# A decoder trunk on one core: low parts of the weights by accumulating transfers, and 17 convolution taps from TensorE to VectorE

## The chip, the core and the metric

The kernel runs on one core of a Trainium2 chip. A core has TensorE for matrix products, VectorE, ScalarE and GpSimd for element-wise work, and SyncE, which here issues transfers; each engine takes its own instructions in order and waits on semaphores. Sixteen DMA engines move data between memory and the on-chip buffer. The metric is the device time of one execution in microseconds, as the median of several runs.

## What is computed

The input is a stream of 512 tokens of 1024 channels, in float32. The first layer is a conformer convolution module and a gated feed-forward, the second an attention with three dilated windows and a feed-forward of the same shape. The conformer module is what the change touches beside the weights:

```python
u = h @ w_in + b_in
u = u[..., :D_MODEL] * jax.nn.sigmoid(u[..., D_MODEL:])
u = causal_dwconv(u, dw, dw_b)        # depthwise, 31 taps
u = layer_norm(u, ln_g, ln_b)         # over the 1024 channels
u = jax.nn.silu(u)
return u @ w_out + b_out
```

Around each module stands a norm before and a norm after with a residual add. The feed-forward has a width of 2816, with a depthwise convolution of three taps; the attention has 8 heads of 128 in each of the three branches.

## The kernel before

**Products.** Activations lie with channels on partitions and tokens along the row. To keep float32 accuracy each operand is split into a high part, rounded to the format of TensorE's fast pass (`F32R`), and a low part, the remainder. A product of x and w is then three products on TensorE: xh·wh, xl·wh and xh·wl (`mm3`), each of 128 × 128 weights with 512 or 256 columns. In names `hh`, `hl` are high and low part of a normed chunk, `sh`, `sl` of the conformer's activated chunk, `whi`, `wlo` of a weight.

**Weights.** The weights come in 240 units of 128 × 1024, in the order of use. `loader` issues a unit's load from SyncE into one of two buffers `raw`, as soon as the low part of the unit two before it has been made. `splitter` makes the high part with a copy on ScalarE and the low part with a subtraction `raw − whi`, on VectorE or on GpSimd, whichever has it sooner by a rough clock; chains of statistics (`self.chains`) keep it off GpSimd. High and low parts have seven buffers each (`RING`), and the splitter runs up to six units (`AHEAD`) before the one in use. Some units are held while their products come in several passes: those of the conformer's output product, of the attention's output product `w_o`, and of a part of the feed-forward. The first two units come in pieces and have their own code (`first_units`).

**Order of the work.** The program is written out by a planner at build time: TensorE's stream leads, and chains of other work (generators) join when a model clock (`Clock`) says that their operands stand. The result is one fixed order for each engine.

**The conformer.** Six of its eight channel chunks are convolved whole, three by banded blocks on TensorE (`T` are the blocks, which GpSimd builds) and three with chains of taps over several engines (`ca`, `cb`, `cacc`). The last two chunks (`MIXES`, 6 and 7) are done in two token halves, in `mix`: of the 30 taps beside the current token, the first 17 of chunk 6 and the first 20 of chunk 7 (`MIX_PE`) are products on TensorE with diagonal matrices (`dh`, `dl`, built by ScalarE; sums in `cm`), three products of 256 columns for each tap and half; the other taps are chained multiply-adds on VectorE (`mc`, 128 × 256 each). Two additions per half bring in the mean `nm` and the products' sum `cm`.

Layer norm follows. `stat_acc` adds three convolved chunks on GpSimd to `m`; TensorE sums its columns (`st`), and the mean, broadcast into `nm`, centres each chunk on VectorE (`d`). The sums of centred values and squares are gathered on GpSimd (`s`), TensorE sums over channels (`lst`), VectorE and GpSimd make the scale (`lnr`), TensorE broadcasts it (`bc`), and VectorE (`ln`, `sl`) and ScalarE (`sh`) make the operands of the output product `wo`. It runs half by half: a0 is the first half of the first four output chunks, b0 their second half.

**Junctions.** Between two modules (`Junction`) the output chunks `y` are squared and summed, a norm is broadcast, and for each chunk VectorE makes `t`, the new residual `x` and the low part `hl`, ScalarE the high part `hh` and squares `sq`, which GpSimd and VectorE add.

The functions that the change touches follow; other functions lost only a comment line.

Of the kernel before, what the change touches and what calls it, by code (L numbers as in the profile page):

```python
# [10 lines left out]
F32 = mybir.dt.float32  # L11
# [14 lines left out]
NEG = -1e30  # L26
RING = 7
AHEAD = 6
SEGS = [list(range(0, 6)), list(range(6, 14)), list(range(14, 22))]
# [3 lines left out]
MIXES = (6, 7)  # L33
MIX_PE = (17, 20)
MAIN_BANKS = 7
TURN = 8
SLACK = 0.3
POOL_BIAS = -1
# [111 lines left out]
class When:  # L150
    """The next step may go once its operands stand and the engine is about to be free."""

# [4 lines left out]
class Meter:  # L157
    """Passes calls on to an engine and keeps a rough clock of when their results stand."""

# [22 lines left out]
class Clock:  # L182
# [55 lines left out]
    def op(self, kind, name, a, k):  # L238
# [3 lines left out]
        if name == "dma_start":  # L242
# [7 lines left out]
            self.free["dma"] = s + n / 360e3  # L250
            fin = self.free["dma"] + 0.9
        else:
# [40 lines left out]
class Junction:  # L293
    """Post-norm, residual add and the operands of the next phase, one token half at a time."""

# [13 lines left out]
    def evict(self, m, p, ap, sl, mode, bias=None, sq=True, after=None, tag=0):  # L309
        """A finished chunk of y leaves PSUM; its squares are summed."""  # L310
        b, nc = self.b, self.b.nc
# [130 lines left out]
class Builder:  # L442
    def __init__(self, tc, ctx, x_d, w_d, vec_d, cvec_d, const_d, out_d):
# [47 lines left out]
        nc.sync.dma_start(self.X[0], x_d[0])  # L491
        self.raw01 = [self.wp.tile([128, 1024], F32, tag="raw", name=self.name("raw"), bufs=2) for _ in range(2)]
        for i, (o0, o1) in enumerate(PIECES):
# [6 lines left out]

    # ---- order of emission: the tensor engine's stream leads, chains of other work join when they are due
    @property
# [47 lines left out]
    def step(self, what):  # L550
        """The main stream waits: time goes on to the next chain that is due."""
        assert self.sides, what
        t = min(s.due(self.clock) for s in self.sides)
        self.now = max(self.now, t)
        assert self.now < self.t + 1000.0 and self.now < 5000.0, what
        self.advance(self.pick(max(t, self.t)))
# [6 lines left out]
    def hold_for(self, *aps):  # L563
        """Chains that are due before the operands stand go first."""
        while self.sides:
            t = self.clock.ready(*aps)
            d = min(s.due(self.clock) for s in self.sides)
            if self.t >= t or d >= t:
                break
            self.step("hold")  # L570
# [4 lines left out]
    def warm(self, out, n):  # L575
        """Products of zeros before the first real ones: the tensor engine's clock is gated down while it idles."""
        for _ in range(n):
            self.nc.tensor.matmul(out[:, :256], self.zero[:, :128], self.zero, start=True, stop=True)

    # ---- tiles  # L580
    def name(self, s):
# [36 lines left out]

    # ---- weights
    def hold(self, specs):  # L620
        """These units stay open until they are released: their products come in several passes."""
        self.held |= {self.index[s] for s in specs}
# [13 lines left out]
    def loader(self):  # L636
        nc = self.nc
        late = [(self.cst0, self.const_d[:, :160]), (self.vec, self.vec_d[:, NVA:]), (self.cst, self.const_d[:, 160:])]
        for u in range(2, len(self.order)):
            yield from self.until(("lo", u - 2))  # L640
            yield At(self.lo_done[u - 2])
            w = self.width(u)
            self.raw[u] = raw = self.wp.tile([128, 1024], F32, tag="raw", name=self.name("raw"), bufs=2)
            self.clock.hold("sp", self.lo_done[u - 2])
            nc.sync.dma_start(raw[:, :w], self.w_d[u, :, :w])
            self.mark(("raw", u))
            if u >= LATE and late:
                nc.sync.dma_start(*late.pop(0))

    def splitter(self):  # L650
        """High parts come from the Activation engine, low parts from whichever of two engines has them sooner."""
        nc, free = self.nc, self.clock.free
        for u in range(2, len(self.order)):
            while u > self.cur + AHEAD or u - RING >= self.oldest or ("raw", u) not in self.flags:
                yield 0.1
            self.next_unit = u
            raw, w = self.raw.pop(u), self.width(u)
            yield When("act", max(self.clock.ready(raw[:, :w]), self.unit_done.get(u - RING, 0.0)), SLACK)
            hi = self.wp.tile([128, 1024], F32R, tag="whi", name=self.name("whi"))
            lo = self.wp.tile([128, 1024], F32R, tag="wlo", name=self.name("wlo"))  # L660
            self.clock.hold("act", self.unit_done.get(u - RING, 0.0))
            nc.scalar.copy(hi[:, :w], raw[:, :w])
            yield self.rdy(hi[:, :w])
            at = self.clock.ready(hi[:, :w])
            if not self.chains and max(free["pool"], at) + w / 476.0 + POOL_BIAS < max(free["dve"], at) + w / 960.0:
                eng = nc.gpsimd
            else:
                eng = nc.vector
                yield self.when("dve", hi[:, :w])
            eng.tensor_tensor(lo[:, :w], raw[:, :w], hi[:, :w].bitcast(F32), op=ALU.subtract)  # L670
            self.lo_done[u] = self.clock.ready(lo[:, :w])
            self.split[self.order[u]] = (hi, lo)
            self.mark(("lo", u))
# [4 lines left out]
    def first_units(self, i):  # L678
        """One piece of the first two units, whose loads are cut so that the first products start early."""
        nc = self.nc  # L680
# [18 lines left out]

    # ---- products  # L700
    def mm3(self, out, wh, wl, xh, xl, start, stop):
# [52 lines left out]

    # ---- statistics
    def sums(self, p, o, accs, blocks):
# [5 lines left out]
    def stat(self, r, acc, blocks, rest=None):  # L762
        """r = (mean square + eps) ** -0.5 of the tokens in the blocks."""
        nc, nb = self.nc, len(blocks)
# [25 lines left out]

    # ---- conformer module
    def conv_taps(self, w_idx, Ts):
        """Banded blocks of the depthwise kernel for tokens taken four at a time."""
        nc = self.nc
# [123 lines left out]
    def stat_acc(self, CO, L):  # L918
        """Sums of the centred channels and of their squares, chunk by chunk as they come."""
        nc = self.nc  # L920
# [362 lines left out]

    # ---- feed-forward
    def ffn(self, layer, Jin, Jout):
# [95 lines left out]

    # ---- attention
    def proj_evict(self, g, p, R, t):
# [330 lines left out]
    def reload(self, src):  # L1714
        """The residual stream comes back from memory: its place was needed for other things."""
        self.X = [self.c2("x") for _ in range(KC)]
# [8 lines left out]
class Chunks:  # L1725
    """Operand pairs looked up when they are needed."""

# [109 lines left out]
```

## Time and profile before

| what | value |
| --- | --- |
| median of 3 runs | 1523.62 us (1523.43 to 1525.43) |
| span of the profiled execution | 1520.0 us |
| the profiled execution's own time beside its span | the page gives none |
| TensorE busy | 1484.2 us, 98% |
| VectorE busy | 941.5 us, 62% |
| ScalarE busy | 603.5 us, 40% |
| GpSimd busy | 355.7 us, 23% |
| loads on SyncE's queue | 135.38 MB |

A busy share is a mean over stages with different limits. The chain of waits goes back from the last instruction to what released it at each step, so it shows which engine set the end where. A row of the timeline gives the start, the time, the instruction with output and inputs, and in brackets the idle time before it with what ended it. In the profile every instruction has the line of the helper that records it (L168), so rows are told apart by engine and by the names of their tiles.

### The profile page before, as it was taken

What the parts mean: (1) busy time and instruction counts of PE and PEld (TensorE: products, weight loads), DVE (VectorE), ACT (ScalarE), POOL (GpSimd) and SP (SyncE); (2) the same over time, 40 slices, a digit from 0 to 9 for tenths busy, and PEclk for the clock granted to TensorE, in tenths of its full rate; (3) what the DMA queues carried; (4) which work ended last, traced back from release to release, by engine and by line L of the source; (5) the groups of instructions that cost most, each with busy time, mean ns of one, the idle gap of its engine ahead of it and who ended that gap; (6) DMA issues with size and microseconds to landing.
All of it is one profiled execution on the core that took longest, in us unless ns stands there. A gap on an engine that the chain in (4) does not pass through costs nothing.

```text
span 1520.0 us, 19689 instructions
## 1 busy us (share of the span) xinstructions
PE 1484.2 (98%) x7778; PEld 1277.0 (84%) x7778; DVE 941.5 (62%) x1366; ACT 603.5 (40%) x1020; POOL 355.7 (23%) x231
## 2 busy tenths in 40 slices
PE   7999999999999998999999999999999999999997
PEld 5889998888888888889888889888898888888887
DVE  7997867846754757722655622566568746754745
ACT  5465564443432425424222323233356334422423
POOL 5885223301210216300000000000044302210213
PEclk9999999999999999999999999999999999999998
DMA  5430322233232322432222232222222332322311
GB/s 183 159 105 29 98 84 84 87 122 97 92 101 84 97 70 86 143 106 96 70 77 77 70 97 84 81 73 70 97 84 84 97 125 84 97 97 91 101 45 56
DMA packets 46892, 139.78 MB, mean 92 GB/s; under 512 B 5072, under 2 KB 10960, under 8 KB 46800
## 3 DMA queue, kind: packets, MB, share of 16 engines
q1 hardware_dynamic: 42768, 135.38, 27.4%
q10 hardware_dynamic: 4032, 3.15, 0.7%
q8 instruction: 61, 1.00, 0.3%
q14 instruction: 31, 0.25, 0.1%
HBM read 132.74 MB, written 5.77 MB: 91 GB/s over the span
## 4 chain that ended last, share of the span: by engine, by line
PE 83%; DVE 5%; ACT 1%; issue 1%; POOL 1%; DMA 0%; POOLq 0%; DVEq 0%; ACTq 0%
PE fi L168 31%; PE kq L168 17%; PE fo L168 16%; PE v L168 9%; PE wo L168 5%; PE sc L168 2%; DVE hl L168 1%; DVE mc L168 1%; DVE x L168 1%; PE pw L168 1%; PE pt L168 1%; PE pv L168 1%; DVE t L168 1%; PE cim L168 1%; PE st L168 0%
## 5 line engine op out<-in xcount | busy, mean ns | idle before, releaser
L168 ACT CAST whi<-raw 128x1024 fp32r<-128x1024 f32 (+2 forms) x242 | 248.2, 1027 | 552.8 <-PE fi L168 175.4
L168 POOL TENSOR_TENSOR wlo<-raw,whi 128x1024 fp32r<-128x1024 f32 (+1 forms) x79 | 190.8, 2416 | 985.8 <-ACT whi L168 975.6
L168 DVE TENSOR_TENSOR wlo<-raw,whi 128x1024 fp32r<-128x1024 f32 (+2 forms) x163 | 206.8, 1269 | 169.0 <-ACT whi L168 168.4
L168 PE MATMUL fi<-hl,whi 128*128 128x512 f32 (+1 forms) x768 | 289.9, 377 | 2.2 <-DVE hl L168 2.2
L168 PE MATMUL fi<-hh,whi 128*128 128x512 f32 (+1 forms) x768 | 290.8, 379 | 0.0
L168 PE MATMUL fi<-hh,wlo 128*128 128x512 f32 (+1 forms) x768 | 289.6, 377 | 0.0
L168 PEld LDWEIGHTS fi<-hl,whi 128*128 128x128 f32 x768 | 145.5, 189 | 31.4 <-DVE hl L168 2.6
L168 PEld LDWEIGHTS fi<-hh,wlo 128*128 128x128 f32 x768 | 145.5, 189 | 28.7
L168 PEld LDWEIGHTS fi<-hh,whi 128*128 128x128 f32 x768 | 145.6, 190 | 28.5
L168 PE MATMUL kq<-hh,whi 128*128 128x512 f32 (+1 forms) x416 | 164.5, 396 | 0.0
L168 PE MATMUL kq<-hh,wlo 128*128 128x512 f32 (+1 forms) x416 | 156.9, 377 | 0.0
L168 PE MATMUL kq<-hl,whi 128*128 128x512 f32 (+1 forms) x416 | 156.7, 377 | 0.0
L168 PE MATMUL fo<-uh,whi 128*128 128x512 f32 (+1 forms) x416 | 150.1, 361 | 0.0
L168 PE MATMUL fo<-uh,wlo 128*128 128x512 f32 (+1 forms) x416 | 149.7, 360 | 0.0
L168 PE MATMUL fo<-ul,whi 128*128 128x512 f32 (+1 forms) x416 | 149.7, 360 | 0.0
L168 DVE SCALAR_TENSOR_TENSOR cc<-z,vec,cc 128x511 f32<-128x511 f32 (+1 forms) x176 | 139.4, 813 | 7.0 <-ACT cc L168 4.3
L168 DVE TENSOR_TENSOR z<-fi,R 128x512 f32<-128x512 f32 x88 | 60.2, 689 | 98.3 <-PE fi L168 96.2
L168 PEld LDWEIGHTS kq<-hh,wlo 128*128 128x128 f32 x416 | 78.3, 188 | 15.5
L168 DVE TENSOR_TENSOR kq<-kq,R 128x512 f32<-128x512 f32 x48 | 46.1, 969 | 70.0 <-PE kq L168 69.3
L168 PEld LDWEIGHTS fo<-ul,whi 128*128 128x128 f32 x416 | 78.3, 188 | 13.1
L168 PEld LDWEIGHTS fo<-uh,whi 128*128 128x128 f32 x416 | 78.3, 188 | 13.0
L168 DVE TENSOR_TENSOR ul<-cc,uh 128x512 fp32r<-128x512 f32 x44 | 75.0, 1705 | 22.7 <-ACT uh L168 22.5
(212 smaller groups left out, 2631.6 us busy)
## 6 DMA issues: line engine op xcount, KB each, us to landing
raw<-in_w_dram SPq DMA_DIRECT2D x222, 512.0 KB, 3.5
raw<-in_w_dram SPq DMA_DIRECT2D x18, 384.0 KB, 3.1
x<-in_x_dram SPq DMA_DIRECT2D x16, 256.0 KB, 4.4
xs<-x SPq DMA_DIRECT2D x8, 256.0 KB, 2.7
x<-xs SPq DMA_DIRECT2D x8, 256.0 KB, 5.1
out_dram<-x SPq DMA_DIRECT2D x16, 128.0 KB, 1.8
ud<-u ACTq DMA_DIRECT2D x3, 256.0 KB, 2.0
ug<-ud ACTq DMA_DIRECT2D x3, 256.0 KB, 3.3
```

Source lines behind the costliest of these rows:

```text
L168: return f(*a, **k)
```

## The change

The low part of a unit is made in another way. ScalarE writes the negative rounded weight, −1 × raw into `wlo`, and copies the rounded weight into `whi` as before; GpSimd then issues a transfer from `raw` to `wlo` that adds what it brings onto what lies there. The buffers for raw weights are four instead of two. Of the diagonal taps 9 and 11 stay on TensorE, where 17 and 20 were; VectorE has 40 taps per half of a chunk pair instead of 23. The model clock gets another figure for transfers issued by GpSimd, which moves the order that it writes. Comment lines that were taken out are not shown.

```diff
+RAWS = 4
-MIX_PE = (17, 20)
+MIX_PE = (9, 11)
...
@@ Clock.op @@
-            fin = self.free["dma"] + 0.9
+            fin = self.free["dma"] + (0.9 if kind != "pool" else 2.0)
...
@@ loader @@
         for u in range(2, len(self.order)):
-            yield from self.until(("lo", u - 2))
-            yield At(self.lo_done[u - 2])
+            if u >= RAWS:
+                yield from self.until(("lo", u - RAWS))
+                yield At(self.lo_done[u - RAWS])
             w = self.width(u)
-            self.raw[u] = raw = self.wp.tile([128, 1024], F32, tag="raw", name=self.name("raw"), bufs=2)
-            self.clock.hold("sp", self.lo_done[u - 2])
+            self.raw[u] = raw = self.wp.tile([128, 1024], F32, tag="raw", name=self.name("raw"), bufs=RAWS)
+            self.clock.hold("sp", self.lo_done.get(u - RAWS, 0.0))
             nc.sync.dma_start(raw[:, :w], self.w_d[u, :, :w])
...
@@ splitter @@
+            nc.scalar.activation(lo[:, :w], raw[:, :w], AF.Copy, scale=-1.0)
             nc.scalar.copy(hi[:, :w], raw[:, :w])
-            yield self.rdy(hi[:, :w])
-            at = self.clock.ready(hi[:, :w])
-            if not self.chains and max(free["pool"], at) + w / 476.0 + POOL_BIAS < max(free["dve"], at) + w / 960.0:
-                eng = nc.gpsimd
-            else:
-                eng = nc.vector
-                yield self.when("dve", hi[:, :w])
-            eng.tensor_tensor(lo[:, :w], raw[:, :w], hi[:, :w].bitcast(F32), op=ALU.subtract)
+            yield self.when("pool", lo[:, :w], slack=0.0)
+            nc.gpsimd.dma_start(lo[:, :w], raw[:, :w], accum_op=ALU.add)
```

What that does to the order is seen in three places. The first place is GpSimd's row at the layer norm of the conformer's second half, where `s` are the sums, `lnr` the scale and `wlo` the weights. Before:

```order
L168 TENSOR_TENSOR s_225_1121<-s_225_1121,sq_1432 128x512
L168 TENSOR_TENSOR s_224_1120<-s_224_1120,mc_962 128x256
L168 TENSOR_TENSOR s_225_1121<-s_225_1121,mq_963 128x256
L168 TENSOR_TENSOR lnr_1509<-lnv_1506,mhalf 128x2
L168 TENSOR_TENSOR wlo_1527<-raw_1036,whi_1526 128x1024
L168 TENSOR_TENSOR wlo_1573<-raw_1500,whi_1572 128x1024
```

And now:

```order
L169 DMA wlo_1400<-raw_842 128x1024
L169 TENSOR_TENSOR s_225_1112<-s_225_1112,d_1357 128x512
L169 TENSOR_TENSOR s_226_1113<-s_226_1113,sq_1422 128x512
L169 DMA wlo_1444<-raw_886 128x1024
L169 TENSOR_TENSOR s_225_1112<-s_225_1112,mc_1010 128x256
L169 TENSOR_TENSOR s_226_1113<-s_226_1113,mq_1011 128x256
L169 DMA wlo_1485<-raw_981 128x1024
L169 TENSOR_TENSOR lnr_1520<-lnv_1517,mhalf 128x2
L169 DMA wlo_1754<-raw_1167 128x1024
```

Issues stand between the sums and ahead of the scale, where subtractions stood behind it. In the same way 12 issues stand ahead of `m` on GpSimd, where four subtractions were.

The second place is TensorE around the sums of the second half, with `wo` the output product and `st`, `lst`, `bc` the sums and the broadcast; in the first listing `sh_1729` is a chunk of the first half, and the sums `lst` stand among products further up, the last 18 of them ahead of the broadcast. Before:

```order
L168 MATMUL wo_1819<-sh_1729,wlo_779 128x256
L168 MATMUL wo_1820<-sh_1729,whi_884 128x256
L168 MATMUL wo_1820<-sl_1730,whi_884 128x256
L168 MATMUL wo_1820<-sh_1729,wlo_885 128x256
L168 MATMUL bc_1928<-cst_75,lnr_1913 128x128 x4
L168 MATMUL wo_1821<-sh_1729,whi_980 128x256
L168 MATMUL wo_1821<-sl_1730,whi_980 128x256
L168 MATMUL wo_1821<-sh_1729,wlo_981 128x256
L168 MATMUL wo_1822<-sh_1729,whi_1472 128x256
L168 MATMUL wo_1822<-sl_1730,whi_1472 128x256
```

And now, with `sh_1738` the last chunk of the first half and `sh_1591` the first of the second:

```order
L169 MATMUL wo_1675<-sh_1738,whi_1399 128x256
L169 MATMUL wo_1675<-sl_1739,whi_1399 128x256
L169 MATMUL wo_1675<-sh_1738,wlo_1400 128x256
L169 MATMUL lst_1850<-ones,s_225_1112 128x1 x2
L169 MATMUL lst_1850<-ones,s_226_1113 128x1 x2
L169 MATMUL lst_1863<-ones,mc_1015 128x1 x2
L169 MATMUL lst_1863<-ones,mq_1016 128x1 x2
L169 MATMUL bc_1876<-cst_75,lnr_1873 128x128 x4
L169 MATMUL wo_1672<-sh_1591,whi_816 128x256
```

Products of the first half stood between the sums and behind the broadcast, 30 of them behind it (6 of this chunk and 24 of the two that follow); now all of them stand ahead of the sums, and b0 follows the broadcast at once.

The third is VectorE at the end of the second half's taps, `mc` of the two chunks, with `nm` and `cm` the mean and the diagonal products. Before:

```order
L168 SCALAR_TENSOR_TENSOR mc_962<-mu_959,vec,mc_962 128x256
L168 TENSOR_TENSOR mc_962<-mc_962,nm_1107 128x256
L168 TENSOR_TENSOR mc_962<-mc_962,cm_1609 128x256
L168 SCALAR_TENSOR_TENSOR mc_967<-mu_964,vec,mc_967 128x256 x3
L168 TENSOR_TENSOR mc_967<-mc_967,nm_1107 128x256
L168 TENSOR_TENSOR mc_967<-mc_967,cm_1695 128x256
L168 TENSOR_SCALAR lns_330_1892<-lst_1877 128x4
```

And now:

```order
L169 SCALAR_TENSOR_TENSOR mc_1010<-mu_1007,vec,mc_1010 128x256
L169 SCALAR_TENSOR_TENSOR mc_1015<-mu_1012,vec,mc_1015 128x256
L169 TENSOR_TENSOR mc_1010<-mc_1010,nm_1098 128x256
L169 TENSOR_TENSOR mc_1010<-mc_1010,cm_1533 128x256
L169 SCALAR_TENSOR_TENSOR mc_1015<-mu_1012,vec,mc_1015 128x256 x5
L169 TENSOR_TENSOR mc_1015<-mc_1015,nm_1098 128x256
L169 TENSOR_TENSOR mc_1015<-mc_1015,cm_1584 128x256
L169 TENSOR_SCALAR lns_324_1857<-lst_1850 128x4
```

The end of the row is the same; ahead of it 17 more taps alternate between the two chunks.

## Rows read from the trace of the kernel before

**Rows 1.** The page, part 1: busy time of the engines

```profile
PE 1484.2 (98%) x7778; PEld 1277.0 (84%) x7778; DVE 941.5 (62%) x1366; ACT 603.5 (40%) x1020; POOL 355.7 (23%) x231
```

**Rows 2.** The page, costliest groups: busy us, mean ns, idle before

```profile
L168 ACT CAST whi<-raw 128x1024 fp32r<-128x1024 f32 (+2 forms) x242 | 248.2, 1027 | 552.8 <-PE fi L168 175.4
L168 POOL TENSOR_TENSOR wlo<-raw,whi 128x1024 fp32r<-128x1024 f32 (+1 forms) x79 | 190.8, 2416 | 985.8 <-ACT whi L168 975.6
L168 DVE TENSOR_TENSOR wlo<-raw,whi 128x1024 fp32r<-128x1024 f32 (+2 forms) x163 | 206.8, 1269 | 169.0 <-ACT whi L168 168.4
```

**Rows 3.** Chain of waits: start us, us, what

```profile
144.64 1.15 PE lst L168 x8
...
180.60 29.54 PE wo L168 x246
...
211.60 1.23 DVE wlo L168
...
226.59 0.94 ACT whi L168
...
339.64 89.23 PE fi L168 x384
...
1136.96 3.00 DVE hl L168 x2
```

**Rows 4.** Windows: length; busy PE, PEld, DVE, ACT, POOL; granted clock, DMA share, GB/s

```profile
164.00:177.00 13.00, 12.21 (x100) 11.71 (x99) 12.45 (x25) 4.49 (x10) 4.24 (x3) 1.00 0.28 102
226.00:228.00 2.00, 0.10 (x1) 0.00 (x0) 2.00 (x5) 2.00 (x5) 0.01 (x1) 1.00 0.01 4
232.00:234.00 2.00, 2.00 (x11) 2.00 (x11) 1.63 (x6) 0.00 (x0) 0.69 (x1) 0.50 0.07 27
```

**Rows 5.** Timeline of GpSimd: start us, us, instruction, idle before

```profile
44.21 2.41 POOL L168 TENSOR_TENSOR wlo<-raw,whi 128x1024 fp32r<-128x1024 f32 x1 [2.20 <-PE cig L168]
...
64.28 6.05 POOL L168 TENSOR_TENSOR T<-cst,cv 128x512 f32<-128x512 f32 x5 [2.67 <-DMA cv<-in_cvec_dram]
...
107.39 1.51 POOL L168 TENSOR_TENSOR m<-m,co 128x512 f32<-128x512 f32 x1
...
178.59 0.71 POOL L168 TENSOR_TENSOR lnr<-lnv,mhalf 128x2 f32<-128x2 f32 x1 [3.05 <-DVE lnv L168]
```

**Rows 6.** Timeline of VectorE: the same columns

```profile
113.64 1.09 DVE L168 TENSOR_TENSOR d<-co,nm 128x512 f32<-128x512 f32 x1 [1.12 <-issue]
...
124.48 3.53 DVE L168 SCALAR_TENSOR_TENSOR mc<-mu,vec,mc 128x230 f32<-128x230 f32 x9
...
141.09 0.42 DVE L168 TENSOR_TENSOR mc<-mc,cm 128x255 f32<-128x255 f32 x1
...
150.73 1.08 DVE L168 TENSOR_TENSOR ln<-d,bc 128x256 f32<-128x256 f32 x3 [1.29 <-PE bc L168]
...
176.40 0.42 DVE L168 TENSOR_TENSOR mc<-mc,cm 128x256 f32<-128x256 f32 x1
...
183.29 0.42 DVE L168 TENSOR_TENSOR sl<-ln,sh 128x256 fp32r<-128x256 f32 x1
...
604.90 1.69 DVE L168 TENSOR_TENSOR wlo<-raw,whi 128x1024 fp32r<-128x1024 f32 x1
...
606.91 1.21 DVE L168 TENSOR_TENSOR wlo<-raw,whi 128x1024 fp32r<-128x1024 f32 x1
...
1124.45 2.44 DVE L168 TENSOR_TENSOR x<-x,t 128x256 f32<-128x256 f32 x1
...
1143.49 0.87 DVE L168 SCALAR_TENSOR_TENSOR hl<-x,vec,hh 128x256 fp32r<-128x256 f32 x2
```

**Rows 7.** The page: DMA queue, and issues with us to landing

```profile
q1 hardware_dynamic: 42768, 135.38, 27.4%
...
raw<-in_w_dram SPq DMA_DIRECT2D x222, 512.0 KB, 3.5
```

**Rows 8.** Timeline of SyncE: one issue of a weight's load

```profile
10.24 0.33 SPq L168 DMA_DIRECT2D raw<-in_w_dram  x1
```

More of the change, by code (lines that the diff above doesn't have):

```diff
@@ L491, in __init__ @@
         nc.sync.dma_start(self.X[0], x_d[0])
-        self.raw01 = [self.wp.tile([128, 1024], F32, tag="raw", name=self.name("raw"), bufs=2) for _ in range(2)]
+        self.raw01 = [self.wp.tile([128, 1024], F32, tag="raw", name=self.name("raw"), bufs=RAWS) for _ in range(2)]
         for i, (o0, o1) in enumerate(PIECES):
```

## The prediction

> **What bounds the kernel now.** I read the busy shares first: TensorE is busy 98% of the span, VectorE 62%, ScalarE 40%, GpSimd 23% [rows 1]. So a change pays where it takes products from TensorE, or where TensorE waits. The costliest groups hold what the change touches: 242 casts on ScalarE, 163 subtractions on VectorE, 79 on GpSimd [rows 2]. The chain of waits says where TensorE itself sets the end (384 products in 89.23 us, 0.232 us per 512 columns; 246 in 29.54 us, 0.120 per 256 columns) and where others stand in for it: the middle of the conformer, on VectorE, and three junctions near 226, 604 and 1140 us, on VectorE and in places on a weight's cast [rows 3]. Then the windows: TensorE is busy for 12.21 of the 13 us from 164 to 177, with VectorE at 12.45, so both engines bound the conformer at nearly the same point; at a junction (226 to 228 us) VectorE and ScalarE have no idle time at all while TensorE rests [rows 4].
>
> **Taps from TensorE to VectorE.** 17 taps, two halves, three products of 256 columns: 102 products, 102 × 0.120 = 12.2 us leave TensorE. That is an upper bound, since the new order stands both layer-norm sums of the second half and their broadcast behind the last product of the first half, where products lay between and behind them before. So TensorE rests until VectorE is through its 40 taps of the second half, and I follow VectorE.
>
> It starts from m, the sum of the channels. Between the first token statistics and m, GpSimd's row holds 12 DMA issues where four subtractions stood, 4 × 2.416 = 9.7 us [rows 2]. An issue on GpSimd is in no row. From below I bound it by SyncE's issue, 0.33 us [rows 8], from above by GpSimd's subtraction, 2.4 us; I take 1.04, GpSimd's smallest arithmetic (0.71) [rows 5] with an issue on top. 12 × 1.04 − 9.7 = +2.8 us of work. GpSimd idles 2.20 and 2.67 us ahead of pieces of this row [rows 5], which can take it up: m, at 107.39 + 1.51 = 108.9 before, comes between 108.9 + 2.8 = 111.7 and 111.7 − 4.9 = 106.8. I take 107, since those pieces wait for others and not for GpSimd; the first centring, 113.64 before, then starts at 111.7 [rows 6].
>
> From there VectorE has 59 instructions to the end of the first half: 40 chained taps at 3.53/9 = 0.392, 15.7 us; six centrings, 1.09 for the first and somewhat less behind it, 4.5; 13 short ones at 0.33, 4.3. That is 24.5 us, to 136.2. Before, the sums of these channels follow the last addition by 3.1 us (141.51 to 144.64) and layer norm of the first half another 6.1 (150.73) [rows 3, 6]; two issues on GpSimd lie between now, 2.1: 136.2 + 3.1 + 2.1 + 6.1 = 147.5. Behind it stand 16 layer-norm steps (1.08/3 = 0.36), 8 low parts (0.42) and an addition, 10.1 us in all (25 at 0.40), and 36 taps at 0.395 (14.2 us): 147.5 + 10.1 + 14.2 = 171.8, where before the last addition ends at 176.82 [rows 6]. From it to the first low part that b0 needs took 183.71 − 176.82 = 6.9 us [rows 6]: b0 starts at 178.7. Before, 30 products of the first half lie behind the broadcast, so b0 starts at 180.60 + 30 × 0.120 = 184.2 [rows 3]. That is −5.5.
>
> TensorE has its other products done by 184.2 − 12.2 = 172.0, rests some 7 us until 178.7, and starts again slower: after such a rest (0.10 us busy from 226 to 228) the granted clock from 232 to 234 is 0.50, that is 1.2 of 2.4 GHz [rows 4]. If 3.4 us pass at that level, 1.7 us are lost; bounds 0 and 3.4. **Conformer: −5.5 + 1.7 = −3.8 us.**
>
> **Low parts by accumulating transfers.** VectorE loses 206.8 us and GpSimd 190.8 us of subtractions, ScalarE gains 238 casts at 1.03, 245 us [rows 2]; none of it is on the path where TensorE is full. A unit's new path is 1.03 us of casting, 1.04 of issuing, and a landing that I take as a load's 3.5 [rows 7] plus one more stream, 1.6: 7.2 us (with a landing between 1.6, its engines' time alone, and 3.5 + 4.8 = 8.3: 3.7 to 10.4), instead of a cast and a subtraction, 1.03 + 1.27 [rows 2]. A ring of seven units, 24 × 0.232 = 5.58 us each, covers that with over 25 us to spare; it shows only where units are held open. In w_o the eighth unit is needed 9 × 0.232 + 30 × 0.120 = 5.7 us after the first is released: 7.2 − 5.7 = **+1.5 us** (bounds 0 and 5). The other two holds give 72 × 0.120 = 8.6 us and more, enough.
>
> The DMA engines: the loads take 27.4% of 1520 us for 135.38 MB, 1.61 us of all sixteen per 512 KB [rows 7]. An accumulating transfer takes 1.6 (one stream) to 4.8 (three); I take 3.2, two streams. Load and accumulate make 4.8 us of the 5.58 that a unit lasts: hidden.
>
> **Junctions.** There VectorE is the chain, and subtractions of weights stand in it that go: 1.2 us (at 211.60), 1.69 + 1.21 = 2.9 (at 604.90), and in the third one like the last, 1.2. Besides, while GpSimd subtracts, VectorE's two low parts of the third take 3.00 us where the next two take 0.87 (−2.1), and an add 2.44 at 1124.45 for some 0.42, of which I count −1.4, since TensorE still has products at that time [rows 3, 6]. Against it, ScalarE has two casts per unit where it had one, and a cast stands in the chain (0.94 at 226.59): 3 × 0.95 = +2.9 us. −1.2 − 2.9 − 1.2 − 2.1 − 1.4 + 2.9 = **−5.9 us**. The most is −8.8, if no cast stands in the chain, the least 0, if the second casts fall ahead of the operands' high parts.
>
> A rule speaks against this term. The Trainium skill ("SBUF — State Buffer", SBUF: two separate sides) says that the descriptors of a DMA from GpSimd are written through the port pair that VectorE shares, and starve while VectorE holds it. The row shows the other direction alone, VectorE slowed by a GpSimd that reads SBUF; no row of before has an issue on GpSimd. By the row I keep −5.9; by the rule the two blocking terms come back, 3.5 us, and this term would be −2.4.
>
> **Sum.** −3.8 + 1.5 − 5.9 = −8.2 us: a span of 1511.8. The page gives the profiled execution no time beside its span of 1520.0; the median of the runs, 1523.62, lies 3.62 above it, so I predict 1515.4 us. A measurement of this kernel can tell 0.2%, 3 us, from no change.
>
> **Rivals.**
> *A, faster still: TensorE stays the bound in the conformer.* If an issue on GpSimd costs about SyncE's 0.33, m and all behind it come some 12 × 0.7 = 8 us sooner, VectorE is through in time, and all products taken away count: −12.2 + 1.5 − 5.9 = −16.6, 1507. For it: issues cost 0.33 on the queue that the trace shows; against it: m also waits for the convolutions, which GpSimd doesn't set. 15%.
> *B, slower: GpSimd's queue.* If an issue costs what a subtraction did, 2.4 us, the 12 issues put 12 × 1.36 = 16.3 us on m, and all of VectorE's row behind it shifts: −8.2 + 16.3 = +8.1, 1532. It turns to a loss from an issue of 1.04 + 8.2/12 = 1.7 us. For it: GpSimd needs 0.71 us even for 128 × 2 elements; against it: SyncE issues in 0.33. 13%.
> *C, slower: the DMA engines become the bound.* With three streams the accumulates take 238 × 4.8 = 1142 us of all engines and the loads 416: 1558 us, and the other queues, the first load and the last products add some 30: 1588. For it: reading two operands and writing one is three streams; against it: a load, a read and a write too, is counted as one 1.6. 7%.
> *D, no change.* ScalarE's second cast falls ahead of the high parts in each junction (0) and the restart costs 3.4: −5.5 + 3.4 + 1.5 = −0.6, 1523. For it: ScalarE's casts are in the chain there already. 17%.
> My forecast, 1509 to 1520.6, has 48%.
>
> **Numbers.** Faster by over 0.2%: the forecast 46, A 15, a piece of D 1: 0.62. Within 0.2%: the forecast's upper end 2 and most of D 15: 0.17. Slower: B, C and a piece of D: 0.21. 1506 to 1530 takes in the forecast, most of A, D and the milder half of B; C lies outside.
>
> **What would show it.** Right: issues on GpSimd near 1 us; loads and accumulates under 90% of the DMA engines' time in a full stretch; TensorE resting until about 179 us, released by VectorE's chain; each junction 1 to 3 us shorter, with VectorE's low parts at 0.87 for two throughout. Wrong: TensorE waiting for low parts in the feed-forward (C); m later than 112 us behind a full GpSimd (B); no rest of TensorE before b0 (A); a weight's cast as what released the high parts in the junctions (D).

## The result, and the profile after

The changed kernel takes 1550.34 us (median of 4 runs, 1548.6 to 1551.39) against 1524.53 of the kernel before in the same series: 1.0166 times as long, with a 95% interval of 1.0152 to 1.018. Forecast were 1515.4 us, and a range of 1506 to 1530. So the change costs some 26 us where I expected it to save 8.

The page of the changed kernel, for [rows 1, 2 and 7]: the span, the busy shares, the groups on the weights, the DMA queues (packets, MB, share of 16 engines) and the median landing in us.

```profile
span 1547.6 us, 19827 instructions
...
PE 1483.3 (96%) x7676; PEld 1270.6 (82%) x7676; DVE 667.4 (43%) x1243; ACT 809.4 (52%) x1227; POOL 354.2 (23%) x389
...
q0 software_dynamic: 34272, 122.70, 43.6%
q1 hardware_dynamic: 42768, 135.38, 27.1%
...
L169 ACT ACTIVATE wlo<-raw 128x1024 fp32r<-128x1024 f32 (+1 forms) x238 | 248.4, 1044 | 462.6 <-PE fi L169 141.2
L169 POOL DMA_DIRECT2D wlo<-raw x238 | 207.0, 870 | 1081.8 <-ACT wlo L169 1050.3
...
raw<-in_w_dram SPq DMA_DIRECT2D x222, 512.0 KB, 4.8
wlo<-raw POOLq DMA_DIRECT2D x222, 512.0 KB, 6.0
```

VectorE is relieved as meant (62% to 43%), and GpSimd's issue takes 0.87 us, near the 1.04 I took. The accumulates' queue takes 43.6% of 1547.6 us for 122.70 MB, 2.9 us of all sixteen engines per 512 KB (3.2 taken). So the single prices of the transfers were right. What went wrong is where they fall, and one other price, that of VectorE's row.

The chain of waits shows it by stages. First two rows of before that [rows 3] does not hold, then those of after that answer to them and to [rows 3] (`wo` 180.60, `fi` 339.64).

```profile
646.36 68.45 PE v L168 x288
...
1249.06 89.60 PE fi L168 x384
```

```profile
22.86 9.66 DMA raw<-in_w_dram
...
45.27 5.85 DMA ud<-u
51.14 4.73 DMA ug<-ud
...
201.05 30.55 PE wo L169 x236
...
354.90 89.60 PE fi L169 x384
...
659.65 68.46 PE v L169 x288
...
1136.61 7.90 DMA raw<-in_w_dram
...
1276.54 89.60 PE fi L169 x384
```

By these marks I divide the kernel: to the first 384 feed-forward products (339.64 before, 354.90 after: +15.3), from there to the first v products (306.72, 304.75: −2.0), on to the second 384 (602.70, 616.89: +14.2), and to the end (270.9, 271.1). Two stretches lose, the conformer and w_o, and the chain shows weight transfers in both. Where TensorE is full nothing is lost, though the DMA engines are busy three times as long (in this view a share of all sixteen can come out a little above 1). These windows are of before and of after (length; PE, PEld, DVE, ACT, POOL; granted clock, DMA share, GB/s):

```profile
0.00:20.00 20.00, 13.21 (x49) 8.11 (x50) 13.40 (x16) 12.57 (x19) 9.86 (x11) 1.00 0.68 233
20.00:40.00 20.00, 18.14 (x83) 14.16 (x82) 15.69 (x18) 8.16 (x10) 14.01 (x10) 1.00 0.43 138
40.00:60.00 20.00, 20.00 (x109) 17.11 (x108) 19.72 (x24) 7.04 (x8) 17.80 (x14) 1.00 0.45 156
...
400.00:450.00 50.00, 50.00 (x217) 40.54 (x216) 32.19 (x35) 18.12 (x22) 10.63 (x4) 1.00 0.29 93
```

```profile
0.00:20.00 20.00, 15.23 (x59) 10.00 (x59) 13.78 (x20) 15.45 (x23) 8.38 (x11) 1.00 0.90 316
20.00:40.00 20.00, 19.19 (x89) 15.32 (x88) 5.73 (x10) 10.23 (x12) 6.44 (x8) 1.00 0.96 236
40.00:60.00 20.00, 11.75 (x51) 9.64 (x50) 19.30 (x22) 12.83 (x16) 17.56 (x20) 0.83 1.01 247
...
180.00:200.00 20.00, 8.83 (x54) 8.04 (x52) 15.82 (x43) 1.75 (x5) 2.45 (x3) 0.73 0.16 41
...
400.00:450.00 50.00, 50.00 (x216) 40.23 (x215) 25.06 (x37) 30.08 (x37) 7.76 (x9) 1.00 0.86 192
...
1141.00:1145.00 4.00, 1.54 (x14) 1.34 (x12) 0.42 (x1) 2.70 (x5) 0.86 (x1) 0.98 1.05 310
1145.00:1150.00 5.00, 0.00 (x0) 0.00 (x0) 0.43 (x1) 5.00 (x11) 3.27 (x3) 0.50 1.08 257
```

From 400 to 450 us TensorE is full in both, with the DMA engines at 0.29 and at 0.86. While the ring of weights is filled, at the start and behind w_o, they are at 0.90 to 1.08, and TensorE rests: it is busy for only 11.75 of 20 us from 40 to 60, and not at all from 1145 to 1150.

How a late transfer gets to TensorE is in ScalarE's timeline of the changed kernel, at the start and behind w_o (idle time before, with what ended it, in brackets):

```profile
32.54 1.06 ACT L169 ACTIVATE wlo<-raw 128x1024 fp32r<-128x1024 f32 x1 [9.74 <-DMA raw<-in_w_dram]
...
1140.72 1.06 ACT L169 ACTIVATE wlo<-raw 128x1024 fp32r<-128x1024 f32 x1 [3.47 <-DMA raw<-in_w_dram]
1141.69 1.03 ACT L169 CAST whi<-raw 128x1024 fp32r<-128x1024 f32 x1
1142.62 0.41 ACT L169 ACTIVATE sq<-y 128x256 f32<-128x256 f32 x1
...
1144.59 1.06 ACT L169 ACTIVATE wlo<-raw 128x1024 fp32r<-128x1024 f32 x1 [1.30 <-DMA raw<-in_w_dram]
...
1149.36 1.16 ACT L169 ACTIVATE sq<-y 128x512 f32<-128x512 f32 x2
1157.39 0.51 ACT L169 ACTIVATE hh<-x,vec 128x256 fp32r<-128x256 f32 x1 [6.88 <-DVE x L169]
```

A cast stands in ScalarE's row and waits for its load; behind it stand, at the start, the copy of the broadcast norm that the conformer's gates need (at 34.44 us, before at 30.46), and behind w_o the squares of the junction's norm, the last at 1149.36, without which the next module's first operand `hh` (1157.39) cannot be made. At the start TensorE still has other products for a while; it stops at the small transfers that regroup the convolved chunks. They come later (`ud` at 45.27 for 41.27) and slower: 5.85 and 4.73 us, where the page of before has these medians, and TensorE waits for them in the changed kernel:

```profile
ud<-u ACTq DMA_DIRECT2D x3, 256.0 KB, 2.0
ug<-ud ACTq DMA_DIRECT2D x3, 256.0 KB, 3.3
```

```profile
56.01 1.62 PE L169 MATMUL cv<-ug,T 128*128 128x128 f32 x6 [8.25 <-DMA ug<-ud]
```

### The profile page after: what moved, and what is told of

The parts are those of the page before. It is cut to its first block, busy times and chain, and to the rows that moved or that the text cites. A ratio compares the mean times of both kernels' runs of the same rounds, so it can differ in the third digit from the quotient of the medians.

```text
span 1547.6 us, 19827 instructions
## 1 busy us (share of the span) xinstructions
PE 1483.3 (96%) x7676; PEld 1270.6 (82%) x7676; DVE 667.4 (43%) x1243; ACT 809.4 (52%) x1227; POOL 354.2 (23%) x389
## 3 DMA queue, kind: packets, MB, share of 16 engines
q0 software_dynamic: 34272, 122.70, 43.6%
## 4 chain that ended last, share of the span: by engine, by line
PE 73%; issue 11%; DVE 7%; DMA 4%; POOL 3%; ACT 2%; SPq 0%; POOLq 0%; ACTq 0%; DVEq 0%
PE fi L169 30%; PE fo L169 16%; PE kq L169 10%; PE v L169 9%; PE wo L169 2%; DMA raw<-in_w_dram 2%; DVE mc L169 2%; DVE x L169 1%; DVE hl L169 1%; POOL wlo L169 1%; DMA wlo<-raw 1%; PE cv L169 1%; DVE t L169 1%; PE sc L169 1%; PE cig L169 1%
## 5 line engine op out<-in xcount | busy, mean ns | idle before, releaser
L169 ACT ACTIVATE wlo<-raw 128x1024 fp32r<-128x1024 f32 (+1 forms) x238 | 248.4, 1044 | 462.6 <-PE fi L169 141.2
L169 POOL DMA_DIRECT2D wlo<-raw x238 | 207.0, 870 | 1081.8 <-ACT wlo L169 1050.3
L169 ACT CAST whi<-raw 128x1024 fp32r<-128x1024 f32 (+2 forms) x242 | 244.6, 1011 | 1.7 <-DMA raw<-in_w_dram 1.5
L169 DVE SCALAR_TENSOR_TENSOR cc<-z,vec,cc 128x511 f32<-128x511 f32 (+1 forms) x176 | 128.2, 749 | 91.5 <-ACT cc L169 88.7
L169 PEld LDWEIGHTS fo<-uh,wlo 128*128 128x128 f32 x416 | 78.2, 188 | 13.2
```

Of the source, the lines that this page charges most:

```text
L169: return f(*a, **k)
```

## The experiments

Theory: wherever the ring of weights is filled anew, a unit's 1.6 + 2.9 us of all DMA engines set the pace, and in-order ScalarE and GpSimd carry that wait to the chains behind them. Rivals: VectorE's 40 taps; the form of the new path (second cast, issue on GpSimd), whatever the transfers take. Times are medians, ratios against the kernel before on the same chip (1524 to 1525 us); the three stretches are from one profile of each.

| kernel | us | ratio (95%) | to first 384 | to v | to second 384 |
| --- | --- | --- | --- | --- | --- |
| before | 1524.5 | 1 | 339.6 | 306.7 | 602.7 |
| changed | 1550.3 | 1.0166 (1.0152, 1.018) | 354.9 | 304.8 | 616.9 |
| e1 taps alone | 1537.6 | 1.0085 (1.0063, 1.0107) | 352.7 | 309.2 | 602.7 |
| e2 accumulates alone | 1548.0 | 1.0154 (1.0122, 1.0186) | 347.2 | 306.3 | 617.9 |
| e3 copy, not add | 1527.8 | 1.0027 (1.0015, 1.0039) | 339.4 | 306.3 | 612.1 |
| e4 planner knows | 1543.7 | 1.0122 (1.0101, 1.0143) | 347.9 | 305.4 | 618.0 |
| e5 subtract to unit 30 | 1548.0 | 1.014 (1.0108, 1.0173) | 346.9 | 306.5 | 619.4 |
| e6 negative on VectorE | 1553.1 | 1.0189 (1.0165, 1.0212) | 367.1 | 307.1 | 606.3 |
| e7 w_o's order | 1540.9 | 1.0109 (1.0088, 1.013) | 357.6 | 306.3 | 605.1 |
| e8 steady part only | 1531.3 | 1.0044 (1.003, 1.0058) | 340.9 | 305.3 | 606.5 |
| e9 both orders | 1529.5 | 1.003 (1.0017, 1.0043) | 348.3 | 304.8 | 604.5 |
| e10 four buffers alone | 1528.3 | 1.0021 (1.0009, 1.0033) | 340.1 | 307.2 | 604.7 |
| e12 copy, w_o's order | 1519.5 | 0.9965 (0.9952, 0.9978) | 337.5 | 306.3 | 603.5 |
| e13 copy in conformer | 1534.6 | 1.0058 (1.0042, 1.0075) | 342.7 | 305.2 | 616.6 |
| e14 e9, two buffers at start | 1539.6 | 1.01 (1.0086, 1.0114) | 353.7 | 306.3 | 605.3 |
| e15 accumulates behind | 1526.9 | 1.0014 (1.0003, 1.0024) | 343.4 | 304.4 | 607.3 |

Kernels whose instructions are the same up to w_o show how far one profile of the conformer can be trusted: 354.9 and 357.6 (changed, e7), 347.9 and 348.3 (e4, e9), but 346.9 and 340.9 (e5, e8). Differences there of less than some 6 us are not read from one profile alone.

**e1, taps alone**

```diff
-MIX_PE = (17, 20)
+MIX_PE = (9, 11)
```

> Taps alone: the kernel before with 9 and 11 diagonal taps on TensorE; low parts by subtraction as before. Theory (refill: the DMA engines are the bound wherever the ring of weights is filled anew, and in-order ScalarE and GpSimd carry that wait to the chains behind them): the conformer's 20 us are not the taps', so 1520 to 1534 us; VectorE gets 34 x 0.39 = 13.3 us more, TensorE 12.2 less. Rival (taps: VectorE's 40 taps per half set the conformer's end): the loss is here, 1540 us or more.

13.1 us to the first 384, just what VectorE's added taps are long (34 × 0.39 = 13.3). With the subtractions still on VectorE they come out in full; at 1537.6 the theory's upper end was 3.6 us too low, and the rival's number is missed by 2.4. So neither is right: the taps do cost in the conformer.

**e2, accumulates alone**

```diff
-MIX_PE = (9, 11)
+MIX_PE = (17, 20)
```

> Accumulating transfers alone: the changed kernel with 17 and 20 diagonal taps on TensorE, as before. Theory (refill): the conformer and the attention's output product lose as in the changed kernel, 1540 to 1555 us. Rival (taps): the conformer's loss of 20 us goes, only the output product's 13 stay against some 7 gained at junctions: about 1530 us.

1548.0: all but 2.3 us of the changed kernel's loss is there by the medians without a single tap moved, w_o's in full. The four runs fall in pairs, near 1544 and near 1552, and the profiled one is of the lower pair; by the profiles the conformer loses 7.6 us here, and 7.7 more when the taps move too. So the taps are not the main cause of the whole loss, but in the conformer their share goes from little, by the medians, to a half, by the profiles; the marks of VectorE's row, in the section on why the prediction was wrong, speak for the half.

**e3, the transfer copies**

```diff
-            nc.gpsimd.dma_start(lo[:, :w], raw[:, :w], accum_op=ALU.add)
+            nc.gpsimd.dma_start(lo[:, :w], raw[:, :w])
```

> The changed kernel, but the transfer from raw to low part copies instead of adding, so the low parts hold the raw weights and the result is another one; issues, waits, sizes and order are the same. Theory (refill): a copy takes the DMA engines about 1.6 us instead of 2.9, a unit 3.2 instead of 4.5, so the refills are a third shorter and most of the loss goes: 1512 to 1530 us. Rival (form: the second cast on ScalarE and the issue on GpSimd in order, whatever the transfer takes): 1545 to 1552 us.

Its page has the same packets and bytes in half the engine time, the issue and the landing shorter:

```profile
q0 software_dynamic: 34272, 122.70, 22.8%
...
L169 POOL DMA_DIRECT2D wlo<-raw x238 | 128.1, 538 | 1131.3 <-ACT wlo L169 1112.6
...
wlo<-raw POOLq DMA_DIRECT2D x222, 512.0 KB, 3.2
```

22 of 26 us go. In the conformer nothing is lost any more (339.4), with the same taps, casts and number of issues: without the adding the conformer does not lose. What the adding changes there is all ahead of the layer norm; the taps' price stays, and an earlier start pays for it (see the section on why the prediction was wrong). A copy is shorter than an adding transfer in three ways at once, on the DMA engines, in its landing and in its issue on GpSimd, and this run doesn't part them; the 12 issues ahead of `m` can make out 12 × 0.33 = 4 us by my estimate. In w_o 9.4 of the 14.2 us stay, so there the form takes part, and the rival has a piece of the truth.

**e4, a planner that knows**

```diff
-            self.free["dma"] = s + n / 360e3
+            self.free["dma"] = s + n * (1.0 if kind != "pool" else 1.8) / 360e3
```

> The changed kernel with a model clock in which a transfer issued by GpSimd keeps the DMA engines busy 1.8 times as long, about as measured, so that the planner puts casts and issues later among the chains' work. Theory (refill, carried by in-order queues): part of the loss is in the order, 1530 to 1545 us. Rival (the transfers' own lateness is all): 1548 to 1553 us; rival (taps): no difference either.

As the theory had it: 1543.7, with 7 us less in the conformer by the same instructions in another order; in w_o nothing.

**e5, subtractions up to unit 30**

```diff
+            acc = u >= 31
...
+            else:
...
+                eng.tensor_tensor(lo[:, :w], raw[:, :w], hi[:, :w].bitcast(F32), op=ALU.subtract)
```

> Subtractions, as before, for the units up to 30 (those of the conformer and of the first refill behind it), accumulating transfers from unit 31 on; 17 and 20 diagonal taps on TensorE. Theory (refill, carried by in-order ScalarE and GpSimd): the conformer is as before (384 products of the first feed-forward start at 339 to 341 us against 347.2 with accumulates alone), the attention's output product still loses 14: 1531 to 1536 us in all. Rival (a constant cost of the accumulates wherever they are): 1541 us or more.

A miss: 1548.0, runs between 1539.7 and 1549.9. That is the rival's number, a constant cost of the accumulates. Its profile loses 16.7 us in w_o and 7.3 in a conformer without accumulates, which e8, with the same instructions there, does not show. Against the rival stands e8, which keeps some four fifths of the accumulates and loses 6.7 us in all. Why the conformer loses here is not shown. Taken by itself the run settles nothing; e13 asks about the conformer with the order unchanged.

**e6, the negative on VectorE**

```diff
-            nc.scalar.activation(lo[:, :w], raw[:, :w], AF.Copy, scale=-1.0)
+            yield self.when("dve", raw[:, :w])
+            nc.vector.tensor_scalar(lo[:, :w], raw[:, :w], -1.0, None, op0=ALU.mult)
```

> The changed kernel, with the negative rounded weight written by VectorE instead of by a second cast on ScalarE. Theory (in w_o some 9 of the 14 us lost are ScalarE's second casts ahead of the junction's squares, the rest the transfers' time): the stretch from the v products to the second 384 products falls from 616.9 to 606 to 610 us, and the conformer loses somewhat less: 1535 to 1543 us. Rival (the transfers' time on the DMA engines alone): the stretch stays at 615 or more, 1547 to 1551 us.

The theory is right for w_o (606.3), where taking ScalarE's second casts away gives back some 10 us. For the whole both numbers are missed, 1553.1: the conformer is 12 us longer still, 10 of them ahead of the first centring (131.96 for 121.68). VectorE now waits in its row for loads as ScalarE did, as here; how much of the 10 us that makes is not shown.

```profile
36.64 0.69 DVE L169 TENSOR_SCALAR wlo<-raw 128x1024 fp32r<-128x1024 f32 x1 [4.12 <-DMA raw<-in_w_dram]
```

**e7, w_o's squares first**

```diff
-            self.spawn(J.evict(m, p, ap, sl, "copy"), 0.9 if m > 3 else 2)
+            self.spawn(J.evict(m, p, ap, sl, "copy"), 0.9)
```

> The changed kernel with one priority changed: in w_o the evictions of the first four chunks rank 0.9 instead of 2, so that ScalarE copies and squares them ahead of the casts of the refill, as in the kernel before. Theory (order on ScalarE): that stretch falls from 616.9 to 606 to 611 us, 1538 to 1544 us in all. Rival (the transfers' time alone): the products behind the refill wait for their weights all the same, 615 or more, 1547 to 1551 us.

1540.9, and 605.1 in the stretch: with the accumulates as they are, another order on ScalarE gives back 11.8 of w_o's 14.2 us. (Copies gave back 4.8 in the old order, so the two overlap.) Its timeline, from the first cast behind the release on:

```profile
1126.51 0.59 ACT L169 COPY y<-wo 128x512 f32<-128x512 f32 x1 [5.34 <-PE wo L169]
1126.99 1.06 ACT L169 ACTIVATE wlo<-raw 128x1024 fp32r<-128x1024 f32 x1
...
1130.37 1.17 ACT L169 ACTIVATE sq<-y 128x512 f32<-128x512 f32 x2
...
1145.35 0.51 ACT L169 ACTIVATE hh<-x,vec 128x256 fp32r<-128x256 f32 x1
```

One unit's casts stand ahead of the first chunks' squares, where in the changed kernel the last of the squares needed stood behind those of seven units. The first operand `hh` of the next module is made at 1145.35, while w_o's last products run; in the changed kernel it was 1157.39, though there w_o's stretch had begun 4.2 us sooner.

**e8, the steady part only**

```diff
-            acc = u >= 31
+            acc = u >= 31 and not WO <= u < WO + 16   # WO = 164, the first unit of w_o
```

> As the first of these four, and subtractions also for the eight units of w_o and the eight behind them: accumulates only where the ring is full and TensorE busy. Theory (refill): neither loss is left, the two junctions' gain of some 2 us may stay: 1518 to 1524 us. Rival (a constant cost): 1532 us or more.

1531.3: 7 us above the theory's number and 0.7 below the rival's. Some four fifths of the accumulates are still there, and a constant cost would have left about that much of the 24 us that e2 loses; 6.7 are left, of which no run shows the cause. It doesn't beat the kernel before.

**e9, both orders mended** (the edits of e4 and e7)

> The changed kernel with both changes of order: a planner that knows the transfers' time, and w_o's squares ahead of the refill's casts. Theory (order carries about half of the loss: 7 us in the conformer, 12 in w_o; the rest is the transfers' time): 1530 to 1535 us. Rival (the two lose the same time twice): 1538 us or more.

1529.5, half a us under the theory's number: of 26 us the two orders take 21 away, with every accumulate and all taps in place.

**e10, four raw buffers in the kernel before**

```diff
-            yield from self.until(("lo", u - 2))
+            if u >= RAWS:   # RAWS = 4, and bufs=RAWS
+                yield from self.until(("lo", u - RAWS))
```

> The kernel before with four buffers for raw weights instead of two and nothing else changed. Theory (the buffers are not what costs): within 3 us of the kernel before. Rival (loads that run further ahead crowd the start, where the first conformer chunks and their small transfers need the DMA engines): 1527 to 1532 us.

1528.3, 3.2 us more: just outside the theory's 3 us and inside the rival's number. So four buffers have a small price of their own, which the changed kernel pays too; it is an eighth of its loss.

**e12, copies and w_o's order** (the edits of e3 and e7)

> The transfer copies instead of adding, as in the earlier run, so the low parts hold raw weights; and w_o's squares stand ahead of the refill's casts. Theory (engine time of the accumulates plus the order in w_o are the whole loss): 1517 to 1522 us, the stretch from the v products to the second 384 at 601 to 604 us. Rival (second cast and issue have a price of their own left): 1526 us or more.

1519.5, 5.6 us faster than before. With the adding's time and w_o's order out of the way nothing of the loss is left; a price of the second casts and of the copies' issues (0.54 us each) is at most hidden in a gain smaller than the 8.2 I had summed. That it comes near that sum is in part luck: `m` ends at 100.18 in it, 7 us ahead of my 107, and VectorE's row is 11.6 us longer than I had it. It leaves the addition out, so it is a measure and no version to use.

**e13, copies for units 2 to 30**

```diff
+            if u < 31:
+                nc.gpsimd.dma_start(lo[:, :w], raw[:, :w])
+            else:
+                nc.gpsimd.dma_start(lo[:, :w], raw[:, :w], accum_op=ALU.add)
```

> The changed kernel, in which the transfers of units 2 to 30 copy instead of adding, so their low parts hold raw weights; from unit 31 on they add; the order is the same throughout. Theory (the conformer loses the engine time of its own accumulates): the first feed-forward's 384 products start at 338 to 343 us as with copies everywhere, not at 354.9, and w_o still loses its 14: 1530 to 1537 us. Rival (the conformer loses by taps, casts and issues): 1545 us or more.

Both as the theory had it: 342.7 to the first 384 and 1534.6 in all. So the transfers of the conformer's own units do it there. The row of its chain, with every instruction ahead of it in the changed kernel's order:

```profile
342.71 89.24 PE fi L169 x384
```

**e14, two raw buffers at the start** (e9, and:)

```diff
-            if u >= RAWS:
-                yield from self.until(("lo", u - RAWS))
+            back = 2 if u < 31 else RAWS
+            yield from self.until(("lo", u - back))
```

> The changed kernel with both changes of order, and loads of units 2 to 30 that wait for the low part two units before, as in the kernel before, instead of four. Theory (the accumulates' own time is what is left in the conformer): 1527 to 1532 us, as with both orders alone. Rival (loads that run ahead crowd the start): 1522 to 1526 us. Second rival (the longer path of a unit, 1 us of casting and 6 of landing, needs the four buffers): 1535 us or more.

1539.6, 10 us slower than e9: the second rival's number. A raw buffer is now held for two casts, an issue and 6 us of landing, and two of them throttle the loads: the DMA engines are busy for 0.65 of the time from 20 to 60 us, in e9 for 0.93 and 1.00. Only 5.4 of the 10 us show in the stretch to the first 384.

**e15, accumulates behind the conformer** (e14 with e5's subtractions, and 17 and 20 taps on TensorE)

> As that kernel, but subtractions for the units up to 30, and 17 and 20 diagonal taps on TensorE: the conformer of the kernel before, accumulates from unit 31 on with the mended orders. Theory (no stretch left with a refill that ScalarE carries ahead of the chains): 1518 to 1523 us, a gain of some 2 us at each of the two later junctions against 1524 to 1525. Rival (the refill behind w_o costs what VectorE's relief gains): 1524 to 1528 us.

1526.9: the rival's number and no gain; the interval lies just above 1. No version with the real addition beat the kernel before.

## Why the prediction was wrong

The step that failed first is the cover for the accumulates: "Load and accumulate make 4.8 us of the 5.58 that a unit lasts: hidden", and "it shows only where units are held open". I compared a unit's DMA time with the time TensorE takes for it, which holds once the ring is full; there it was right (50.00 of 50 us busy). While a ring of seven is filled, units are wanted as fast as they come, and seven times 4.5 us is 31 us by estimate where seven loads alone are 11. I had reckoned that for the last unit of w_o alone, as a landing that is 1.5 us late, and left out the first filling, at the start of the kernel, and the queues that stall behind it. A second step failed beside it, the 24.5 us of VectorE: the instructions were counted right and priced wrong. The third is w_o's +1.5. Against the kernel before, the conformer's 15.3 us come about half from the first and half from the second, and w_o's 14.2 mostly from order.

These marks of the conformer tell the first two steps apart (us; VectorE's row goes from the start of the first centring to the end of the last addition of the first half; in the kernels with 40 taps these are the 59 instructions of the prediction):

| kernel | `m` ends | first centring | VectorE's row | to first 384 |
| --- | --- | --- | --- | --- |
| before | 108.9 | 113.6 | 27.9 | 339.6 |
| forecast | 107 | 111.7 | 24.5 | |
| changed | 117.5 | 121.7 | 36.0 | 354.9 |
| e2 accumulates alone | 118.6 | 122.9 | 30.7 | 347.2 |
| e3 copy, not add | 101.8 | 106.0 | 36.0 | 339.4 |
| e13 copy in conformer | 105.7 | 109.9 | 36.0 | 342.7 |

Three rows of the changed kernel, and the same three of e3:

```profile
115.54 1.91 POOL L169 TENSOR_TENSOR m<-m,co 128x512 f32<-128x512 f32 x1
...
121.68 1.09 DVE L169 TENSOR_TENSOR d<-co,nm 128x512 f32<-128x512 f32 x1
...
157.31 0.42 DVE L169 TENSOR_TENSOR mc<-mc,cm 128x255 f32<-128x255 f32 x1
```

```profile
99.88 1.91 POOL L169 TENSOR_TENSOR m<-m,co 128x512 f32<-128x512 f32 x1
...
106.02 1.08 DVE L169 TENSOR_TENSOR d<-co,nm 128x512 f32<-128x512 f32 x1
...
141.63 0.42 DVE L169 TENSOR_TENSOR mc<-mc,cm 128x255 f32<-128x255 f32 x1
```

The adding puts `m`, and the first centring behind it, 15.7 us later than copies do, and changes nothing in VectorE's row. With the 17 taps that row is 8.2 us longer than before and 5.3 longer than in e2 (where VectorE also waits 2.60 us in it for the last convolved chunk), whether transfers add or copy; with copies a first centring 7.6 us earlier than before pays for it, so the conformer comes out even. That is why taking the adding away wins back all 15.3 us, though only about half of them are its own.

- *Prices.* Issue 0.87 (1.04), accumulate 2.9 (3.2), landing 6.0 (5.1): all inside their bounds. Rival B's price of 2.4 did not come; rival C's mechanism did, in two places and not throughout.
- *m at 107.* It ended at 115.54 + 1.91 = 117.45, past the 112 that I had named as a sign of rival B, but not behind a full GpSimd: GpSimd is busy for 16.13 of the 20 us from 80 to 100 and 12.88 from 100 to 120, and its last issue ahead of `m` had waited 6.34 us for ScalarE's cast. The chain of waits leads from a load at 22.86 over the cast at 32.54, the small transfers and the banded products, which I had not followed, to `m`. I had cost an issue as time and not as a wait.
- *24.5 us of VectorE behind m.* It took 36.0, of which VectorE idles 0.83 up to the last centring. I had priced the taps at 0.39 us from a stretch where GpSimd was quiet. Beside GpSimd's sums they are slower: three taps take 3.26 us while two sums run, and 24 take 9.81 with GpSimd at rest. Before, this stretch took 27.9 us with 17 taps fewer and some taps of other chunks in it; my rows held that (113.64 to 141.51, [rows 6]), and I did not use it. The last convolved chunk was not what VectorE waited for: its transfer was issued at 140.9 and landed 2.7 us later, while its centring stood behind the 24 taps until 150.20.

```profile
131.42 3.26 DVE L169 SCALAR_TENSOR_TENSOR mc<-mu,vec,mc 128x243 f32<-128x243 f32 x3
...
140.47 9.81 DVE L169 SCALAR_TENSOR_TENSOR mc<-mu,vec,mc 128x236 f32<-128x236 f32 x24
```

```profile
131.64 1.37 POOL L169 TENSOR_TENSOR s<-s,d 128x512 f32<-128x512 f32 x1 [1.40 <-DVE d L169]
132.97 1.44 POOL L169 TENSOR_TENSOR s<-s,sq 128x512 f32<-128x512 f32 x1
```

- *Behind it the count was fair.* From the first half's layer norm (167.09) to the last addition (193.09) 26.0 us, 24.3 taken; from there to the start of the first low part of b0 7.5 (200.59), where it took 6.5 before. b0 starts at 201.05 instead of 178.7: 10.4 of these 22.4 us are `m`, 11.5 VectorE's row.
- *The rest before b0.* It came, longer than thought: TensorE is busy for 8.83 of 20 us from 180 to 200, at a granted clock of 0.73, so partly at the lower of its two levels, as [rows 4] show it for another rest. Behind the start of b0 the clock stays at 0.50 for some 5 us, so some 2.6 us are lost by estimate; I had 1.7, from 3.4 us for which I had shown no row.
- *w_o, +1.5.* Measured +14.2, the junction's forecast gain included: 11.8 of it by order (e7), since the planner put the last of the junction's squares behind the casts of seven units, and 2.4 left. That second casts can hold up a junction I had as a gain that shrinks (rival D), not as a loss.
- *Junctions, −5.9 for three.* From the low part of b0 to the first 384 products 154.3 us for 156.4, and 2.0 less in the second stretch: −4 us in the two that aren't w_o's, where the sum had −2.2. That agrees with the mechanism, but does not show it: the second stretch varies from 304.4 to 307.1 among the kernels with transfers. w_o's junction, with the larger part of the −5.9, gained nothing in any run. The Trainium skill's rule on descriptors that starve ("SBUF — State Buffer", SBUF: two separate sides) was not tested by a run of its own. The issue is longer for an accumulate (0.87) than for a copy (0.54) at the same VectorE load, so I can't read its length as starving.
- *Taps, −12.2 as an upper bound.* Not reached: even with copies the conformer gains 2 us at most (e12).

In e9, with both orders mended, the conformer still loses 8.7 us: the first centring is 3.7 late (117.31) and VectorE's row 5.1 longer (33.0). Open: what of the adding's price in the conformer is the engines' time, what its longer landing and what its longer issue; and why one profile of the same conformer can differ by 6 us (e5, e8).

## What to carry to other kernels

Compare a new transfer with the pace at the places where buffers are refilled, not with the steady pace, and follow what stands behind each waiting instruction on its in-order engine. Work taken off a busy engine and put on an idle one still costs if it stands in that engine's row ahead of something that the critical engine needs; a change of order alone gave back 21 of 26 us here. When a planner writes the order, give it the measured time of the new operation first (e4). And price added work on an engine from a stretch that has the same neighbours busy: 17 taps at 0.39 us, taken with GpSimd quiet, missed what the row really takes beside GpSimd's sums.

## What the runs showed of the hardware

An accumulating transfer of 512 KB within the on-chip buffer took 2.9 us of all sixteen DMA engines, a plain copy of the same packets 22.8% of 1528.8 us for 122.70 MB, 1.5 us; so adding costs about one more stream. The Trainium skill ("Collectives: The Full Stack", The bandwidth ceiling: the fold count and why AG ≠ RS ≠ AR) explains the halved rate of a collective that adds by two source reads for the add. The ratio of 1.9 here agrees with that; no run here counts the reads. An accumulate's issue on GpSimd took 0.87 us where a copy's took 0.54, and its median landing 6.0 us where the copy's took 3.2. Three of VectorE's taps of 128 × 243 took 3.26 us beside two of GpSimd's sums of 128 × 512, and 24 of them 9.81 us without.
